# One more seven-product pair in each channel mixer, an accumulating transfer for a second operand sum, and all five engines' orders from one list scheduler

## The chip, the cores and the metric

The kernel runs on one core of a Trainium2 chip. The time is the device time of one execution in microseconds (us); three executions of the kernel before gave 562.88, 563.20 and 563.69 us, so the median is 563.2 us. The engines are named as in the profile: PE (TensorE matmul), PEld (its weight load), DVE (VectorE), ACT (ScalarE), POOL (GpSimd) and SP (SyncE, which here only issues loads).

## The reference

A two-layer decoder trunk on 256 positions of width 1024, in fp32. Layer 0 mixes tokens with a chunked gated MLP, layer 1 with causal attention; in both, four heads attend in parallel to 256 memory tokens. Then each layer has a dense channel mixer:

```python
def swiglu(x, w_in, w_out):
    g, u = jnp.split(x @ w_in, 2, axis=-1)
    return (jax.nn.silu(g) * u) @ w_out

for i in range(DEPTH):                 # 2 layers
    ...                                # mix = gmlp or attention, mem_out = memory attention
    sub = jnp.concatenate([mix, mem_out], axis=-1) @ w_mix_out[i]
    x = layer_norm(ALPHA * x + sub, ln_mix_g[i], ln_mix_b[i])
    x = layer_norm(ALPHA * x + swiglu(x, w_ffn_in[i], w_ffn_out[i]), ln_ffn_g[i], ln_ffn_b[i])
return x
```

The hidden width is 2816, that is 11 chunks of 256 hidden cells; a chunk of `w_in` has 1024 rows and 512 columns (256 for the gate g, 256 for u).

## The kernel before, in words

**Precision.** Every large product is computed from two halves of each operand: ACT writes a rounded `hi` (L248), DVE subtracts it from the source for `lo` (L249), and PE runs three passes, hi·hi, hi·lo and lo·hi, into the same PSUM tile (`PASSES`, L272). So each weight of 128x2048 that comes in by DMA costs two ACT casts and two DVE subtractions of 128x1024, called a split below; the two halves of one weight carry a 0 or a 1 in their name (`spl_s_4_M_0_...` is half 0 or 1 of some product's operand of pair 4; the digit before the last number is the half).

**Channel mixer.** A chunk is computed in one of two ways (`PLANS`, `ffn_steps`). A plain block R multiplies the four row groups of its weight, for both 128-position token tiles: 4x2x3x2 = 48 matmuls of 128x512. A pair S takes two chunks together, cuts positions and rows in two, and computes the 2x2 block product with seven products, M1 to M7, instead of eight: 7x12 = 84 matmuls where two plain blocks take 96. The price is in the operands. Four sums of the token side are made once per layer (`sums`, the tiles `SfM`, `SgM`). On the weight side the host has combined the blocks into four raw tiles per pair, `11`, `12`, `21` and `22`, and four of the seven products need a sum of two of them: M5 = 11+12, M6 adds 22 to that, M7 = 12+22, M4 = 21 + the running sum in 11. The results build up in three PSUM tiles: X takes M1, M6, M7 and M4 one after the other, Y takes M2, Z takes M5 and M3. ACT copies X after M1, Z after M5 and X after M6 to SBUF (`m1`, `m5`, `u2`), DVE adds Y to m1 (L625), Z to u2 (L629) and X to m5 (L632), and after the silu of each half one DVE instruction makes the hidden values (L630, L636). After four transposes per chunk (`transposes`, L658), made during the next block, they are split into `ht` and are the stationary side of the out-product (`chunk_out`, tiles `fof` in layer 0 and `fog` in layer 1).

Before, each layer has three plain blocks and four pairs, and a pair's products run in the order M1, M5, M2, M3, M6, M7, M4. The sums for M5, M6 and M4 are DVE additions of 128x2048 (L199). The sum for M7 is a DMA that POOL issues (L202): it reads `22` from HBM once more and adds it to the `12` in SBUF while writing. All four sums of a layer's token side, and the transposes of the second token tile, stand in the step `x`; in layer 1 the plain blocks 0 and 1 are cut by token tile around it, so that PE has work while the second tile's layer norm runs.

**Order.** Weights come through `Stream`: SP loads raw tiles of 1 MB in the order of use, four rotating buffers and two fixed ones for `11` and `21` (`TAGS`); `make` sums and splits them into ten rotating half tiles (`HALF_BUFS`). PE runs in the order in which the program is written (`manual_schedule`). The other engines are ordered by the framework's scheduler, except for some splits that `stream.behind` holds back.

Of the kernel before, what the change touches and what calls it, by code (L numbers as in the profile page):

```python
# [34 lines left out]
RAW_BUFS = 4  # L35
# [8 lines left out]
PLANS = ((("R", 0), ("R", 1), ("S", 2), ("S", 4), ("S", 6), ("S", 8), ("R", 10)),  # L44
         (("R", 0), ("R", 1), ("R", 2), ("S", 3), ("S", 5), ("S", 7), ("S", 9)))
PRODUCTS = ("M1", "M5", "M2", "M3", "M6", "M7", "M4")

OPERAND = {"M1": ("11", None), "M5": ("11", "12"), "M2": ("21", None), "M3": ("22", None),
           "M6": ("11", "22"), "M7": ("12", "22"), "M4": ("21", "11")}
TAGS = {"11": "gb", "21": "vbig"}  # L50


def ffn_steps(l):

    steps, due, prev = [], [], []
    for kind, c in PLANS[l]:
        new = [("out", p, k, (0, 1)) for p in prev for k in range(2)]
        if kind == "S":


            ins = [("s", c, m) for m in PRODUCTS]
            due += new
            early, due = due[:-3], due[-3:]
            if c == NFF - 2:

                steps += [ins[0], ("tp",), *early, *ins[1:5], due[0], ins[5], ("out", c - 1, 0, (0,)), ("turn", c, 0),
                          ("out", c - 1, 1, (0,)), ins[6]]
                continue
            steps += [ins[0], ("tp",), *early[:1], ins[1], *early[1:], *ins[2:5], due[0], ins[5], due[1], ins[6]]
            due = due[2:]  # L70
        else:
            ins = [("r", c, i, (0, 1)) for i in range(4)]
            if l == 1 and c == 0:

                steps += [*(("r", 0, i, (0,)) for i in range(4)), *(("r", 1, i, (0,)) for i in range(2)), ("x",)]
            elif l == 1 and c == 1:
                steps += [*(("r", 1, i, (0,)) for i in range(2, 4)), *(("r", 0, i, (1,)) for i in range(4)),
                          *(("r", 1, i, (1,)) for i in range(2)), ("tp",), *(("r", 1, i, (1,)) for i in range(2, 4))]
                due += new
            elif c == NFF - 1:  # L80
                steps += [ins[0], ("tp",), *due, *ins[1:], *(("out", NFF - 3, k, (0,)) for k in range(2)), ("tp",)]
            elif c:
                steps += [ins[0], ("tp",), *ins[1:]]
                due += new
            else:
                steps += ins
        prev = [c, c + 1] if kind == "S" else [c]
    return steps


# [971 lines left out]
```

## Time and profile before

The profiled execution has a span of 561.0 us from its first to its last instruction; the three timed executions have a median of 563.2 us. No device time beside the span is given for the profiled execution itself, so the 2.2 us between the two are taken as lying around the span.

| of the span of 561.0 us | busy us | share | instructions |
|---|---|---|---|
| PE | 550.9 | 98% | 3052 |
| PEld | 478.4 | 85% | 3052 |
| DVE | 500.5 | 89% | 667 |
| ACT | 360.1 | 64% | 550 |
| POOL | 22.4 | 4% | 32 |

The granted TensorE clock is 0.998 over the span. Loads that SP issues take 52.8% of the 16 DMA engines' time, the transfers that POOL issues 8.1%. How to read it: PE has work almost without a gap, DVE is full in parts of the span and not in others, so a mean over the span says little of either; each part of the program has to be looked at for itself.

### The profile page before, as it was taken

What the parts mean: (1) busy time and instruction counts of PE and PEld (TensorE: products, weight loads), DVE (VectorE), ACT (ScalarE), POOL (GpSimd) and SP (SyncE); (2) the same over time, 40 slices, a digit from 0 to 9 for tenths busy, and PEclk for the clock granted to TensorE, in tenths of its full rate; (3) what the DMA queues carried; (4) which work ended last, traced back from release to release, by engine and by line L of the source; (5) the groups of instructions that cost most, each with busy time, mean ns of one, the idle gap of its engine ahead of it and who ended that gap; (6) DMA issues with size and microseconds to landing.
All of it is one profiled execution on the core that took longest, in us unless ns stands there. A gap on an engine that the chain in (4) does not pass through costs nothing.

```text
span 561.0 us, 8037 instructions
## 1 busy us (share of the span) xinstructions
PE 550.9 (98%) x3052; PEld 478.4 (85%) x3052; DVE 500.5 (89%) x667; ACT 360.1 (64%) x550; POOL 22.4 (4%) x32
## 2 busy tenths in 40 slices
PE   8999999999999999999999999999999999999994
PEld 8999979888888888888899999788888887888883
DVE  5897999999998999995987879789998997999985
ACT  6766947767655766863466879765676674765910
POOL 2020000000000000000000000000000000000001
PEclk9999999999999999999999999999999999999999
DMA  8997794548756486598477222367258766485602
GB/s 291 399 324 308 250 369 170 208 77 313 210 206 247 112 325 161 192 335 296 140 240 297 75 77 76 142 254 280 85 152 316 197 249 217 133 307 145 225 1 75
DMA packets 21623, 118.88 MB, mean 212 GB/s; under 512 B 2384, under 2 KB 6096, under 8 KB 9168
## 3 DMA queue, kind: packets, MB, share of 16 engines
q1 hardware_dynamic: 20000, 109.45, 52.8%
q0 software_dynamic: 1152, 8.39, 8.1%
q8 instruction: 24, 0.39, 0.3%
q10 hardware_dynamic: 432, 0.52, 0.3%
q14 instruction: 15, 0.12, 0.1%
HBM read 117.31 MB, written 1.05 MB: 211 GB/s over the span
## 4 chain that ended last, share of the span: by engine, by line
PE 85%; DVE 7%; ACT 3%; DMA 2%; issue 2%; SPq 1%; DVEq 0%; ACTq 0%
PE fof L272 11%; PE fog L272 8%; PE Xf L272 8%; PE pg L272 6%; PE pf L272 6%; PE Xg L272 5%; PE opc L272 4%; PE opa L272 4%; PE Zf L272 4%; PE qk L272 4%; PE pu L272 3%; PE bv L272 3%; PE Zg L272 3%; PE pvm L272 3%; PE va L272 2%; PE hkm L272 2%
## 5 line engine op out<-in xcount | busy, mean ns | idle before, releaser
L248 ACT CAST spl_s_M<-raw_s 128x1024 fp32r<-128x1024 f32 x112 | 114.4, 1052 | 56.7 <-DVE raw_s L199 41.9
L249 DVE TENSOR_TENSOR spl_s_M<-raw_s,spl_s_M 128x1024 fp32r<-128x1024 f32 x112 | 132.6, 1217 | 7.7 <-ACT spl_s_M L248 7.5
L272 PE MATMUL fof<-spl_w,htf 128*128 128x512 f32 x264 | 63.8, 392 | 0.0
L272 PE MATMUL fog<-spl_w,htg 128*128 128x512 f32 (+1 forms) x282 | 63.7, 378 | 0.0
L272 PEld LDWEIGHTS fog<-spl_w,htg 128*128 128x128 f32 x282 | 50.2, 188 | 9.4
L272 PEld LDWEIGHTS fof<-spl_w,htf 128*128 128x128 f32 x264 | 49.0, 188 | 10.0
L199 DVE TENSOR_TENSOR raw_s<-raw_s,raw_s 128x2048 f32<-128x2048 f32 x24 | 54.8, 2284 | 0.2
L249 DVE TENSOR_TENSOR spl_w<-raw_w,spl_w 128x1024 fp32r<-128x1024 f32 x44 | 53.0, 1217 | 1.2 <-ACT spl_w L248 1.1
L248 ACT CAST spl_w<-raw_w 128x1024 fp32r<-128x1024 f32 x44 | 45.4, 1050 | 4.7 <-PE fog L272 1.9
L272 PE MATMUL qk<-x2T,spl_qk 128*128 128x256 f32 x288 | 36.3, 283 | 0.0
L272 PEld LDWEIGHTS qk<-x2T,spl_qk 128*128 128x128 f32 x288 | 35.2, 192 | 0.0
L272 PE MATMUL Xf<-spl_s_M,SfM 128*128 128x512 f32 x96 | 23.1, 389 | 0.0
L272 PE MATMUL opc<-spl_o,mix 128*128 128x512 f32 x96 | 23.1, 394 | 0.0
L272 PE MATMUL Zf<-spl_s_M,SfM 128*128 128x512 f32 x96 | 23.1, 389 | 0.0
L272 PE MATMUL Zg<-spl_s_M,SgM 128*128 128x512 f32 x96 | 23.1, 389 | 0.0
L272 PE MATMUL Xg<-spl_s_M,SgM 128*128 128x512 f32 x96 | 23.1, 389 | 0.0
L272 PE MATMUL Xg<-spl_s_M,x3T 128*128 128x512 f32 x96 | 22.7, 391 | 0.2 <-DVE m5g L632 0.2
L272 PE MATMUL Xf<-spl_s_M,x1T 128*128 128x512 f32 x96 | 22.6, 389 | 0.0
L272 PE MATMUL opa<-spl_o,mix 128*128 128x512 f32 x96 | 22.5, 392 | 0.0
L272 PEld LDWEIGHTS Xg<-spl_s_M,x3T 128*128 128x128 f32 x96 | 17.9, 188 | 4.4 <-DVE m5g L632 0.6
L272 PEld LDWEIGHTS Xf<-spl_s_M,SfM 128*128 128x128 f32 x96 | 18.0, 188 | 3.8
L272 PEld LDWEIGHTS Xg<-spl_s_M,SgM 128*128 128x128 f32 x96 | 18.0, 188 | 3.7
(245 smaller groups left out, 1080.2 us busy)
## 6 DMA issues: line engine op xcount, KB each, us to landing
raw_s<-in_w SPq DMA_DIRECT2D x32, 1024.0 KB, 5.1
raw_w<-in_w SPq DMA_DIRECT2D x22, 1024.0 KB, 4.8
raw_o<-in_w SPq DMA_DIRECT2D x8, 1024.0 KB, 6.3
raw_s<-in_w POOLq DMA_DIRECT2D x8, 1024.0 KB, 7.9
raw_r_A<-in_w SPq DMA_DIRECT2D x6, 1024.0 KB, 4.9
raw_r_B<-in_w SPq DMA_DIRECT2D x6, 1024.0 KB, 6.0
raw_qk<-in_w SPq DMA_DIRECT2D x6, 1024.0 KB, 5.5
raw_u<-in_w SPq DMA_DIRECT2D x3, 1024.0 KB, 9.2
```

The costliest lines, as they stand in the source:

```text
L199: self.nc.vector.tensor_add(self.raw[parts[0]], self.raw[parts[0]], self.raw[parts[1]])
L248: nc.scalar.copy(hi, src)
L249: nc.vector.tensor_sub(lo, src, hi.bitcast(F32))
L272: nc.tensor.matmul(o, lhsT, rhs, start=start, stop=stop, skip_group_check=on)
```

## The change

Both layers now have one plain block (chunk 0) and five pairs (1, 3, 5, 7, 9). The order of a pair's products is M1, M5, M2, M6, M3, M7, M4. Of the four weight sums, M5 and M6 stay DVE additions; M7 is still loaded from HBM with an accumulating transfer (now issued when M7's own half is made, not with M5's), and M4 is an accumulating transfer too, from the SBUF tile `11` into the SBUF tile `21`. For the pairs after the first, M1 is copied from X to Y within PSUM and M2 accumulates on top of it, so the silu reads Y and the DVE addition of L625 goes away. A number of copies may run on ACT or on DVE (`nc.copy`, `nc.scale`). The two fixed raw buffers join the rotating ones (six in all), and other tiles that stood in them (x0raw, gv, vn, vt, the layer norm's rows) take such a slot too. Layer 0 now ends as layer 1 did before: on a pair whose second half is turned in the tail (`turn_tile`).

The order of all five engines is now manual. The program is recorded as a list (`Plan.add`); PE keeps the order in which the program is written, `deadlines` works back from it to a latest start for each other instruction, `simulate` lays the instructions out five times with five sets of limits and a table of assumed costs, and the layout in which PE loses least is emitted.

```diff
-RAW_BUFS = 4
+RAW_BUFS = 6
 HALF_BUFS = 10
...
-PLANS = ((("R", 0), ("R", 1), ("S", 2), ("S", 4), ("S", 6), ("S", 8), ("R", 10)),
-         (("R", 0), ("R", 1), ("R", 2), ("S", 3), ("S", 5), ("S", 7), ("S", 9)))
-PRODUCTS = ("M1", "M5", "M2", "M3", "M6", "M7", "M4")
+PLANS = ((("R", 0), ("S", 1), ("S", 3), ("S", 5), ("S", 7), ("S", 9)),) * 2
+PRODUCTS = ("M1", "M5", "M2", "M6", "M3", "M7", "M4")
...
+LOADED = ("M7",)
+MOVED = ("M4",)
...
+        if l == 1 and c == 1:
+
+            first, second = ([("r", 0, i, (tt,)) for i in range(4)] for tt in range(2))
+            steps += [ins["M1"], first[0], ins["M2"], first[1], ("x",), *first[2:], *second, ins["M5"], ("tp",), ins["M6"],
+                      ins["M3"], ins["M7"], due[0], ins["M4"]]
+            due = due[1:]
+        elif c == NFF - 2:
+
+            steps += [ins["M1"], ("tp",), *early, ins["M5"], ins["M2"], ins["M6"], ins["M3"], due[0], ins["M7"],
+                      ("out", c - 1, 0, (0,)), ("turn", c, 0), ("out", c - 1, 1, (0,)), ins["M4"]]
         else:
...
+            n = 2 if early else 1
+            steps += [ins["M1"], ("tp",), *early[:1], ins["M5"], *early[1:], ins["M2"], ins["M6"], ins["M3"], *due[:n - 1],
+                      ins["M7"], due[n - 1], ins["M4"]]
+            due = due[n:]
...
     def make(self):
...
-        if len(parts) == 2 and key[-1] == 0:
+        if key[1] in MOVED and key[-1] == 0:
+            self.nc.gpsimd.dma_start(self.raw[parts[0]], self.raw[parts[1]], accum_op=ALU.add)
+        elif len(parts) == 2 and key[-1] == 0:
             self.nc.vector.tensor_add(self.raw[parts[0]], self.raw[parts[0]], self.raw[parts[1]])
-            if key[1] == "M5":
-                a, b = (f"{key[0]}_{q}" for q in OPERAND["M7"])
-                self.nc.gpsimd.dma_start(self.raw[a], self.unit_ap(b), accum_op=ALU.add)
+        if key[1] in LOADED and key[-1] == 0:
+            a, b = (f"{key[0]}_{q}" for q in OPERAND[key[1]])
+            self.nc.gpsimd.dma_start(self.raw[a], self.unit_ap(b), accum_op=ALU.add)
...
-        tc.manual_schedule(engines={ET.PE}),
+        tc.manual_schedule(engines={ET.PE, ET.DVE, ET.Activation, ET.Pool, ET.SP}),
...
                 if m == "M1":
-                    self.m1 = kept("m1", self.X)
+                    if self.Y.whole:
+                        nc.copy(self.Y, self.X)
+                    else:
+                        self.m1 = kept("m1", self.X)
...
-                    nc.vector.tensor_add(self.m1, self.m1, self.Y)
-                    nc.scalar.activation(self.m1, self.m1, AF.Silu)
+                    if self.Y.whole:
+                        self.m1 = work_tile(f"m1{self.nm}{c}")
+                        nc.scalar.activation(self.m1, self.Y, AF.Silu)
...
                 elif m == "M6":
-                    u2 = kept("u2", self.X)
-                    nc.vector.tensor_add(u2, u2, self.Z)
-                    nc.vector.scalar_tensor_tensor(self.m1, self.m1, -1.0, u2, ALU.mult, ALU.mult)
+                    self.u2 = kept("u2", self.X)
+                elif m == "M3":
+                    nc.vector.tensor_add(self.u2, self.u2, self.Z)
+                    nc.vector.scalar_tensor_tensor(self.m1, self.m1, -1.0, self.u2, ALU.mult, ALU.mult)
...
-            if i == 2:
-                gb = load_gb(1, "mix")
...
+        gb = [load_row(tile_of("act", [P, D], F32, "klm", "g1mix"), 1, "mix_g")]
...
+        gb.append(load_row(tile_of("act", [P, D], F32, "klq", "b1mix"), 1, "mix_b"))
...
+    def either(self, a, b):
+
+        op = self.add(*a)
+        op.other = Op(op.n, *b)
+
+    def copy(self, out, src):
+        self.either(("scalar", "copy", (out, src), {}), ("vector", "tensor_copy", (out, src), {}))
...
+    def deadlines(self):
+        t = 4300
+        for op in self.ops:
+            if op.engine == "tensor":
+                op.late = t
+                t += op.hold
...
+        for op in reversed(self.ops):
+            late = [o.late - self.delay(op, o) for o in op.after if o.late is not None]
+            late += [follow[b].late - self.delay(op, follow[b]) for b in op.roots if b in follow]
+            if op.late is not None:
+                late.append(op.late)
+            op.late = min(late) if late else t
...
+        for trial in self.TRIALS:
...
+            out, lost = self.simulate(*trial)
+            self.trials.append(lost)
+            if best is None or lost < best[0]:
+                best = lost, [(op, op.opens, op.call, op.start, op.end, [b.slot for b in op.opens]) for op in out]
...
+                t0 = min(t for t, _ in c)
+                first = [x for x in c if x[0] <= t0 + 1]
+                t, op = min(first, key=lambda x: (x[1].late, x[1].n))
```

Three places show how the instructions move. The first is POOL over layer 0's channel mixer. Before it issues one transfer per pair, all of them from `in_w` in HBM:

```order
L362 TENSOR_TENSOR rsa_1047<-rsa_1047,mhalf 128x1
L202 DMA raw_s_2_12_1294<-in_w 128x2048
L202 DMA raw_s_4_12_1591<-in_w 128x2048
L202 DMA raw_s_6_12_1826<-in_w 128x2048
L202 DMA raw_s_8_12_2061<-in_w 128x2048
```

Now it issues two per pair, one from `in_w` and one from the SBUF tile `raw_s_..._11`:

```order
L520 TENSOR_TENSOR rsa_1108<-rsa_1108,mhalf 128x1
L520 DMA raw_s_1_12_923<-in_w 128x2048
L520 DMA raw_s_1_21_1006<-raw_s_1_11_870 128x2048
L520 DMA raw_s_3_12_1394<-in_w 128x2048
L520 DMA raw_s_3_21_1432<-raw_s_3_11_1171 128x2048
L520 DMA raw_s_5_12_1644<-in_w 128x2048
L520 DMA raw_s_5_21_1668<-raw_s_5_11_1636 128x2048
```

The second place is DVE towards the end of a pair of layer 0, with the sum for M4 before (pair 4; `raw_s_4_21` is the target, `htf` the split of transposed hidden values, `spl_w` the splits of out-weights):

```order
L249 TENSOR_TENSOR spl_s_4_M_0_1777<-raw_s_4_12_1591,spl_s_4_M_0_1777 128x1024
L249 TENSOR_TENSOR spl_s_4_M_1_1786<-raw_s_4_12_1591,spl_s_4_M_1_1786 128x1024
L249 TENSOR_TENSOR spl_w_3_0_1796<-raw_w_3_1650,spl_w_3_0_1796 128x1024
L199 TENSOR_TENSOR raw_s_4_21_1595<-raw_s_4_21_1595,raw_s_4_11_1589 128x2048
L625 TENSOR_TENSOR m1f_1631<-m1f_1631,Yf_1611 128x512
L249 TENSOR_TENSOR spl_s_4_M_0_1812<-raw_s_4_21_1595,spl_s_4_M_0_1812 128x1024
```

Now, in pair 5, from the split of M2's operand (the last reader of the old `21`) to the first split of the sum that the transfer leaves in the same tile:

```order
L520 TENSOR_TENSOR raw_s_5_11_1636<-raw_s_5_11_1636,raw_s_5_22_1696 128x2048
L520 TENSOR_TENSOR spl_s_5_M_0_1726<-raw_s_5_21_1668,spl_s_5_M_0_1726 128x1024
L520 TENSOR_TENSOR spl_s_5_M_1_1757<-raw_s_5_21_1668,spl_s_5_M_1_1757 128x1024
L520 TENSOR_TENSOR spl_s_5_M_0_1812<-raw_s_5_11_1636,spl_s_5_M_0_1812 128x1024
L520 TENSOR_TENSOR spl_s_5_M_1_1819<-raw_s_5_11_1636,spl_s_5_M_1_1819 128x1024
L520 TENSOR_TENSOR spl_s_5_M_0_1765<-raw_s_5_22_1696,spl_s_5_M_0_1765 128x1024
L520 TENSOR_TENSOR spl_s_5_M_1_1772<-raw_s_5_22_1696,spl_s_5_M_1_1772 128x1024
L520 TENSOR_TENSOR spl_w_3_1_1804<-raw_w_3_1664,spl_w_3_1_1804 128x1024
L520 TENSOR_TENSOR spl_s_5_M_0_1826<-raw_s_5_12_1644,spl_s_5_M_0_1826 128x1024
L520 TENSOR_TENSOR spl_s_5_M_1_1839<-raw_s_5_12_1644,spl_s_5_M_1_1839 128x1024
L520 TENSOR_TENSOR spl_w_4_0_1848<-raw_w_4_1746,spl_w_4_0_1848 128x1024
L520 TENSOR_TENSOR htf_1794<-tpf_1779,htf_1794 128x512
```

The row that follows the last one is `spl_s_5_M_0_1894<-raw_s_5_21_1668`, the split that needs the landed sum. The addition of 128x2048 has gone from between; nine other instructions lie between the second row of `21` and that split.

The third place is PE at the start of layer 1's channel mixer, from the first matmul that needs only the first token tile (`ptc` are the transposes of the second tile, `pg` the plain blocks). Before:

```order
L272 MATMUL pg_3780<-spl_r_0_A_3777,x3T 128x512 x6
L272 MATMUL pg_3780<-spl_r_0_A_3787,x3T 128x512 x6
L272 MATMUL pg_3780<-spl_r_0_B_3798,x3T 128x512 x6
L272 MATMUL pg_3780<-spl_r_0_B_3807,x3T 128x512 x6
L272 MATMUL pg_3826<-spl_r_1_A_3823,x3T 128x512 x6
L272 MATMUL pg_3826<-spl_r_1_A_3833,x3T 128x512 x6
L374 MATMUL ptc_3844<-ident,xres 128x128 x4
L374 MATMUL ptc_3853<-ident,xres 128x128 x4
L272 MATMUL pg_3826<-spl_r_1_B_3882,x3T 128x512 x6
L272 MATMUL pg_3826<-spl_r_1_B_3891,x3T 128x512 x6
```

Now M1 and M2 of pair 1 stand among the pieces of the plain block, and behind the plain block's second tile comes M5 (`Zg`), the first product that needs the token sums `SgM`:

```order
L520 MATMUL Xg_3810<-spl_s_1_M_0_3538,x3T 128x512 x6
L520 MATMUL Xg_3810<-spl_s_1_M_1_3574,x3T 128x512 x6
L520 MATMUL pg_3835<-spl_r_0_A_3703,x3T 128x512 x6
L520 MATMUL Yg_3846<-spl_s_1_M_0_3712,x3T 128x512 x6
L520 MATMUL Yg_3846<-spl_s_1_M_1_3738,x3T 128x512 x6
L520 MATMUL pg_3835<-spl_r_0_A_3753,x3T 128x512 x6
L520 MATMUL ptc_3877<-ident,xres 128x128 x4
L520 MATMUL ptc_3882<-ident,xres 128x128 x4
L520 MATMUL pg_3835<-spl_r_0_B_3763,x3T 128x512 x6
L520 MATMUL pg_3835<-spl_r_0_B_3774,x3T 128x512 x6
L520 MATMUL pg_3908<-spl_r_0_A_3703,x3T 128x512 x6
L520 MATMUL pg_3908<-spl_r_0_A_3753,x3T 128x512 x6
```

Two pieces of `r_0_B` follow, and then `Zg_3955<-spl_s_1_M_0_3805,SgM_3918`. Before, the pieces of two plain blocks for both token tiles and then a whole third plain block stood ahead of the first product on `SgM`; now it is one plain block with M1 and M2.

More of the change, by code (lines that the diff above doesn't have):

```diff
@@ L56, in ffn_steps @@
     for kind, c in PLANS[l]:
[L57 to L70, printed above, removed]
-        else:
[L72 to L86, printed above, removed]
@@ new lines, with __init__ @@
+class Buffer(View):
+    def __init__(self, pool, space, tag, bufs, shape, dtype, name):
+        n = 1
+        for s in shape[1:]:
+            n *= s
+        ap = space[:P * n].rearrange("(p n) -> p n", p=P)
+        if len(shape) > 2:
+            names = "abcd"[:len(shape) - 1]
+            ap = ap.rearrange(f"p ({' '.join(names)}) -> p {' '.join(names)}", **dict(zip(names, shape[1:])))
+        super().__init__(None, ap)
+        self.pool, self.tag, self.bufs, self.dims, self.dtype, self.name = pool, tag, bufs, list(shape), dtype, name
+        self.psum, self.whole = pool == "ps", False
+        self.tile, self.log, self.slot, self.left, self.last = None, [], None, 0, 0.0
@@ new lines, with __init__, calls, cost @@
+class Op:
+    def __init__(self, n, engine, name, args, kw):
+        self.n, self.engine, self.name, self.args, self.kw = n, engine, name, args, kw
+        out = kw["out"] if "out" in kw else args[0]
+        views = [v for v in [*args, *kw.values()] if isinstance(v, View)]
+        self.writes = [v for v in (out, kw.get("accum_out")) if isinstance(v, View)]
+        self.reads = [v for v in views if not any(v is w for w in self.writes)]
+        self.before, self.after, self.opens = {}, [], []
+        self.late, self.other = None, None
+        self.cost()
+    def calls(self):
+        return {o.engine: o for o in (self, self.other) if o}
+    def cost(self):
+        w = max([v.width() for v in self.writes + self.reads] or [1])
+        e, n = self.engine, self.name
+        if n == "dma_start":
+            v = (self.writes or self.reads)[0]
+            self.bytes = 4 * v.ap.ap[0][1] * v.width()
+            self.hold, self.lat = (900 if e == "gpsimd" else 400), 0
+        elif e == "tensor":
+            w = self.args[2].width() if n == "matmul" else P
+            f32 = n == "matmul" and self.args[2].root.dtype == F32
+            self.hold = max(104, (w + 32) / 2.4) if not f32 else 0.85 * w
+            self.lat = 200 + 0.37 * w if not f32 else self.hold + 270
+        elif e == "vector":
+            slow = n in ("tensor_scalar_mul", "tensor_scalar_add") or n == "tensor_copy"
+            self.lat = 225 + 0.48 * w if n == "tensor_scalar_mul" and w > 8 else 150 + 1.042 * w
+            self.hold = self.lat - 82
+        elif e == "scalar":
+            self.lat = 190 + 0.842 * w + (200 if "accum_out" in self.kw else 0)
+            self.hold = self.lat - 100
+        else:
+            self.lat = self.hold = 700 + 2.5 * w if w < 8 else 250 + 2.0 * w
@@ L293, in build @@
             pattern=[[0, 2], [-1, P]], channel_multiplier=1)
-        klm, klq = (const.tile([P, 2, 2, T], F32R, name=n) for n in ("klm", "klq"))
+        klm, klq = (tile_of("act", [P, 2, 2, T], F32R, n, n) for n in ("klm", "klq"))
         for kl in (klm, klq):
@@ L493, in mem_q @@
         def mem_q(name, xs):
-            qa = [actp.tile([P, 2, T], F32R, tag=f"qm{c}", name=f"q{name}{c}") for c in range(2)]
+            qa = [tile_of("act", [P, 2, T], F32R, f"qm{c}", f"q{name}{c}") for c in range(2)]
             t = proj_t(name, xs)
```

443 lines of the change are left out of this document (363 added, 80 removed).

## The prediction

> **What bounds the kernel now.** I read the page's busy line first, then what PE waited for, then the chain of waits for the spacing of PE's work, then the windows for DVE.
>
> ```profile
> span 561.0 us, 8037 instructions
> PE 550.9 (98%) x3052; PEld 478.4 (85%) x3052; DVE 500.5 (89%) x667; ACT 360.1 (64%) x550; POOL 22.4 (4%) x32
> ```
>
> ```profile
> PE warmup L284 <- DVE mhalf L281: 1.1, 1, 1.1
> PE va L272 <- ACT spl_v L248: 0.6, 1, 0.6
> PE s L272 <- DVE klq L480: 0.6, 2, 0.4
> PE Xg L272 <- DVE m5g L632: 0.2, 1, 0.2
> ```
>
> The list of PE's waits has four entries, 2.5 us in all, and the first two belong to the start. PE is the bound: 0.8 us in the middle (0.6 + 0.2) is all that a better order could win back there. What remains is the amount of PE work, and whether the others keep up with less of it. Two stretches of the chain give the price of PE work:
>
> ```profile
> 132.21 2.72 PE Yf L272 x12
> ...
> 153.97 0.87 PE tpf L658 x8
> ...
> 184.79 0.87 PE tpf L658 x8
> ```
>
> Twelve matmuls of 128x512 take 2.72 us, 0.2267 us each. From one pair's transposes to the next pair's are 30.82 us: 7 products and 4 pieces of out-product, 11 x 2.72 + 0.87 = 30.8. So a pair runs on PE with no gap. Beside it stands DVE:
>
> ```profile
> core 0: us, PE busy (x) PEld busy (x) DVE busy (x) ACT busy (x) POOL busy (x), PEclk, DMA share, GB/s
> 140.00:160.00 20.00, 20.00 (x94) 16.67 (x93) 20.00 (x20) 12.75 (x17) 0.87 (x1) 1.00 0.60 164
> 440.00:460.00 20.00, 20.00 (x93) 16.61 (x93) 20.00 (x19) 13.00 (x16) 0.00 (x0) 1.00 0.68 217
> ```
>
> ```profile
> L249 DVE TENSOR_TENSOR spl_s_M<-raw_s,spl_s_M 128x1024 fp32r<-128x1024 f32 x112 | 132.6, 1217 | 7.7 <-ACT spl_s_M L248 7.5
> L199 DVE TENSOR_TENSOR raw_s<-raw_s,raw_s 128x2048 f32<-128x2048 f32 x24 | 54.8, 2284 | 0.2
> L249 DVE TENSOR_TENSOR spl_w<-raw_w,spl_w 128x1024 fp32r<-128x1024 f32 x44 | 53.0, 1217 | 1.2 <-ACT spl_w L248 1.1
> L632 DVE TENSOR_TENSOR m5f<-m5f,Xf 128x512 f32<-128x512 f32 x4 | 2.7, 680 | 0.0
> ```
>
> In the pairs DVE is full as well. Per instruction (busy over count, since neighbours overlap a little) a split is 132.6/112 = 1.184 us, an out-weight split 53.0/44 = 1.205, a weight sum 54.8/24 = 2.28, a 512-wide step 2.7/4 = 0.675. A pair needs 14 splits, 4 out-weight splits, 3 sums and 7 steps: 16.6 + 4.8 + 6.8 + 4.7 = 33.0 us, against PE's 30.8. DVE falls behind by some 2 us per pair and lives on the lead won in the plain blocks (48 matmuls, 10.9 us of PE, for only 4 splits, 4.7 us).
>
> **The change part by part.**
>
> *PE.* A layer goes from 3 x 48 + 4 x 84 to 48 + 5 x 84 matmuls of 128x512: 480 to 468. Over two layers that is 24 fewer, 24 x 0.2267 = **5.44 us less**. Out-products and transposes keep their number.
>
> The Trainium skill ("Perfetto Trace Analysis", Identifying the Most-Contended Engine) says that matmul busy time judges TensorE badly and weight-load busy time should be used. The row for that is
>
> ```profile
> L272 PEld LDWEIGHTS fof<-spl_w,htf 128*128 128x128 f32 x264 | 49.0, 188 | 10.0
> ```
>
> and by it 24 matmuls would be worth 24 x 0.188 = 4.5 us; the starts in the chain above are 0.2267 apart with no gap, so the trace goes with 5.44.
>
> *Waits in the middle.* The 0.6 us on klq and the 0.2 on m5g came from DVE's order. The new order has every latest start in view; I take back all of it, **-0.8** (bounds 0 and -0.8).
>
> *DVE inside a pair.* One sum fewer (M4, -2.28), the addition of Y gone (-0.675), and a copy here and there that was ACT's (about half a step per pair): 21.4 + 2 x 2.28 + 6.5 x 0.675 = 30.4 us, against 30.8. So five pairs in a row, with no plain block between to recover, should hold with 0.4 us to spare each, where the old load would have lost 5 x 2.2 = 11 us of lead. This is the step on which the gain stands. Price 0. Bounds: 0, and 2.7 (the new order has 15 copies on DVE where there were 6; five of the nine are counted here, the other four at 0.675 could fall where DVE has no lead). ACT is 64% busy, and its 14 added casts hide in its idle third:
>
> ```profile
> L248 ACT CAST spl_s_M<-raw_s 128x1024 fp32r<-128x1024 f32 x112 | 114.4, 1052 | 56.7 <-DVE raw_s L199 41.9
> ```
>
> Without that cover each would cost 1.05 us.
>
> *The transfers of the sums.* Per pair POOL now issues two, and they have these rows:
>
> ```profile
> raw_s<-in_w POOLq DMA_DIRECT2D x8, 1024.0 KB, 7.9
> ...
> q1 hardware_dynamic: 20000, 109.45, 52.8%
> q0 software_dynamic: 1152, 8.39, 8.1%
> ```
>
> ```profile
> 146.19 0.87 POOL L202 DMA_DIRECT2D raw_s<-in_w  x1 [30.53 <-DVE raw_s L199]
> ```
>
> ```profile
> DMA to landing us min/median/max: 7.8/7.9/9.0
> ```
>
> M7's sum has some 15 DVE instructions between its release and its first split, about 17 us against 0.9 + 7.9: safe. For M4 the transfer may start when M2's split has read the old `21`, and must have landed for the split nine DVE instructions later (the second place of the order): 8 splits and one `htf`, 8 x 1.184 + 0.675 = 10.1 us, against 0.9 of issue and 7.9 of landing. The margin is **1.3 us**. An accumulating transfer out of SBUF is not in this trace; the nearest row is the one from HBM, 7.8 to 9.0. I take 7.9, so price 0. The DMA engines have room: a load of 1 MiB costs 2.84 us of them (52.8% of 561.0 over 109.45 MB), an accumulating one 5.68 (8.1% over 8.39 MB), so a pair used 6 x 2.84 + 5.68 = 22.7 of its 30.8 us and will use 28.4, 92%. That leaves room, but a load that meets both will land later than now. Bounds: 0, and 2.0 us per pair (rival C).
>
> *Start of layer 1's channel mixer.* One plain block instead of three has to cover the second tile's layer norm and the token sums.
>
> ```profile
> 374.37 0.87 PE ptc L374 x8
> 377.98 8.17 PE pg L272 x36
> 386.15 0.87 PE ptc L374 x8
> ```
>
> ```profile
> L366 DVE SCALAR_TENSOR_TENSOR xres<-xres,rsc,gb1mix 128x512 f32<-128x512 f32 x4 | 2.8, 745 | 0.0
> L353 DVE BATCH_NORM_STATS2 stc<-xres 128x6 f32<-128x512 f32 x4 | 2.6, 679 | 0.0
> L596 DVE TENSOR_TENSOR hg<-hg,pg 128x256 f32<-128x256 f32 x6 | 2.5, 414 | 0.2
> ```
>
> Count from the first matmul on the first tile alone (377.98 now). A piece of six is 8.17/6 = 1.36. M1, piece, M2, piece, transposes, two pieces, four pieces of the second tile: 2.72 + 1.36 + 2.72 + 1.36 + 0.87 + 2.72 + 5.44 = 17.2. Then M5, four transposes, M6, M3 and M7's first half: M7's second half is due at 27.15. By then DVE has to do the layer norm (five of 0.70, two of 0.65, small ones: 5.0), 10 splits (11.8), a weight sum (2.3), 12 steps (8.1) and two `hg` (0.8): 28.0. Short by about **1.0**, and I take that. Bounds: 0 (if copies go to ACT), and 3.0 (four more 0.675 steps of the sums on DVE's path). Layer 0's start has no such squeeze: its whole first block is plain and the same work stands behind both tiles; 0.
>
> *Hand-offs.* At a pair's end the silu of X, the product with m5 and the transposes must fit behind the next M1, 2.72 us; one of them already shows a wait.
>
> ```profile
> 473.33 0.61 DVE m5g L632
> 473.98 5.74 PE Xg L272 x24
> ```
>
> There are ten of them now and eight before. New is the copy of X into Y, which must be there before M2 writes on it: M5 and an out-product piece lie between, at least 2.72 us, for one step of about 0.7, on ACT or DVE. If that cover is gone, PE waits the step itself. I take **0.5** for all hand-offs; bounds 0 and 5.6 (a 0.7 step late in each of the eight pairs with such a copy).
>
> *Ends and start.* Layer 0 now ends in a turned half, as layer 1 does, where PE runs through without a wait:
>
> ```profile
> 536.41 2.74 PE Xg L272 x12
> 539.15 2.72 PE fog L272 x12
> 542.31 11.18 PE fog L272 x66
> ```
>
> Between the last two rows lie 0.44 us, four transposes at 0.11. Price 0; if the second half's split came late there, one step of 0.675 is the bound. The tail behind it is unchanged in its steps. At the start SP's loads stand in another order (v1's first piece ahead of v0's last half): 0, bounds 0.6 either way, the size of PE's wait for spl_v above. The rows for layer 1's first norm are loaded later, into space of klm and klq:
>
> ```profile
> gb1mix<-in_ln_mix_b SPq DMA_DIRECT2D x1, 512.0 KB, 4.9
> ```
>
> A landing of 4.9 us is covered by the six out-product pieces ahead of the close, over 8 us; 0.
>
> *Sum on the span:* 561.0 - 5.44 - 0.8 + 1.0 + 0.5 = 556.3, that is 4.7 less. The median of the runs is 2.2 above the span, so 563.2 - 4.7 = **558.5 us**.
>
> **The rivals.**
>
> *A, the forecast:* PE stays the bound, DVE just holds. Own range 556.5 (no loss at all: 563.2 - 6.2 = 557.0, and the 0.6 of the start) to 560.5 (the bounds of start and hand-offs half used).
>
> *B, the gain is half eaten by order.* DVE is strict in its order and 99% full (30.4 of 30.8) for five pairs; a late cast or landing now has no plain block behind it to make up for. For it: DVE's rows are 7.5 us idle behind ACT's casts in `spl_s_M` alone, 7.5/112 = 0.07 us each, 0.9 us per pair if they lay inside the pairs, which is more than the spare 0.4: 10 x 0.5 = 5 us less what the lead of ten half tiles buffers. Against: those waits fell mostly where DVE was ahead. Half of it, 2.5 us, gives 561.0.
>
> *C, slower: M4's transfer lands late.* Place: the pairs. DVE stops at the split of `21`, and everything behind it (the next pair's splits, then PE) moves. The point from which it decides: the 10.1 us less 0.9 of issue allow a landing of 9.2; DVE's spare of 0.4 makes it 9.6; and ten half tiles, worth 1.36 us of PE each, hold some 10 us of lead at the start of a layer's pairs, 2 us for each of the five, so 11.6. For it: two loads ahead of it in the DMA engines would make 7.9 + 2 x 2.84 = 13.6, and loads do spread:
>
> ```profile
> DMA to landing us min/median/max: 4.7/5.9/9.0
> ```
>
> Then a pair loses 13.6 - 11.6 = 2.0; in four of the ten pairs 8.0: 561.0 + 8.0 - 5.4 - 0.8 + 1.0 = 563.8 on the span, **566**. Against: the eight POOL transfers land within 7.8 to 9.0, with the DMA engines 0.60 to 0.68 busy in the windows above.
>
> The Trainium skill ("SBUF — State Buffer", two separate sides) warns of a trap in which a DVE instruction holds the port that GpSimd needs to write descriptors, so that transfers issued by POOL wait. The issues here took 0.87 us in a stretch where DVE was 20.00 of 20.00 busy, so the trace does not bear it out for these DVE instructions; what would be added is at most one DVE instruction, 1.2 to 2.3 us, per issue.
>
> *D, no change:* the new order keeps DVE too far ahead or behind at the layers' starts (3.0) and the hand-offs lose 2.5: 557.0 + 5.5 = 562.5.
>
> **How the numbers follow.** A 0.62, B 0.18, C 0.13, D 0.07. The time is A's, 558.5. The range leaves A's lower edge in and goes up through B and D to the lower part of C: 556.0 to 565.0; beyond it lies most of C. The measurement can tell 0.2%, 1.1 us, from no change, so faster is below 562.1: A and nearly all of B and a little of D, 0.78. The same is D's middle and B's end, 0.08; slower, above 564.3, is C and D's upper end, 0.14.
>
> **What would show it.** 24 fewer PE matmuls and a PE busy time near 545.5; no entry above 0.5 us in PE's waits except the start's, one at `Zg` or `Xg` of layer 1's first pair of about 1 us. DVE near 20 of 20 in every window of the pairs, and at most small waits of DVE on a transfer. Landing of POOL's transfers at 8 to 9 us. Wrong is the forecast if PE waits in the later pairs of a layer for splits (B), if ACT or DVE wait for `raw_s` DMAs and landings reach 11 us (C), or if the PE spacing in the pairs is no longer 2.72 per product.

## The result, and the profile after

The changed kernel takes 570.3 us, the kernel before 563.45 us beside it: ratio 1.0141, 95% interval 1.0111 to 1.0171. It is slower by 6.9 us where 4.7 us less was forecast; the median lies above the stated range (556.0 to 565.0). The profiled execution has a span of 568.1 us, 7.1 more than before.

The page of the changed kernel, as of before: the span and the busy time of each engine.

```profile
span 568.1 us, 8070 instructions
PE 550.0 (97%) x3028; PEld 475.2 (84%) x3028; DVE 506.1 (89%) x674; ACT 370.8 (65%) x563; POOL 32.7 (6%) x44
```

PE has the 24 matmuls less (3052 to 3028), but its busy time fell by 0.9 us, not by 5.4. So PE now waits, and some of its matmuls run slower. The list of PE's waits (what PE waited for: us in total, times, longest) says where:

```profile
PE tpg L520 <- DVE m5g L520: 2.9, 3, 2.0
PE tpf L520 <- DVE m5f L520: 1.5, 1, 1.5
PE qk L520 <- DVE mix L520: 1.2, 1, 1.2
PE tpf L520 <- DVE hf L520: 1.2, 1, 1.2
PE Xf L520 <- DVE m5f L520: 1.2, 1, 1.2
PE warmup L674 <- DVE mhalf L671: 1.1, 1, 1.1
PE Zg L520 <- DVE htg L520: 0.6, 1, 0.6
PE tpg L520 <- DVE m1g L520: 0.6, 1, 0.6
```

Before, the list had four entries and 2.5 us; now it has ten and 11.0 us. Seven of the eight shown are new, and six of them are hand-offs of the channel mixer: the transposes `tpf` and `tpg` wait for the hidden values m1, m5 and hf, the next products for what is made of them.

The first matmul of each stage in the two traces shows in which stage the 12.5 us went (7.1 more, where 5.4 less of work is done). The channel mixers have 2.72 us less work each.

| stage | before, us | after, us | lost against its work |
|---|---|---|---|
| up to layer 0's channel mixer | 101.07 | 101.70 | 0.6 |
| layer 0's channel mixer | 174.78 | 177.14 | 5.1 |
| layer 1's attention | 101.97 | 102.41 | 0.4 |
| layer 1's channel mixer, to the end of PE's last matmul | 175.66 | 179.80 | 6.9 |
| the tail behind PE | 7.49 | 7.01 | -0.5 |

What is late for the hidden values is seen in the chain of waits of the changed kernel, here through a pair of layer 1 (start, us, what):

```profile
459.80 2.28 DVE spl_s_M L520 x2
...
462.71 7.74 DMA raw_s<-raw_s
...
471.28 10.39 DMA raw_s<-in_w
...
484.62 1.05 ACT spl_s_M L520
485.67 0.49 ACT sgg L520
...
486.19 0.70 DVE m5g L520
486.89 0.05 issue
486.93 0.98 PE tpg L520 x7
```

Read it from above: DVE splits M2's operand; that releases M4's transfer (7.74 us); its landing frees a raw slot, for which SP has a load waiting; that load lands 10.39 us after its issue; its casts stand on ACT ahead of the silu `sgg`; the product m5 comes after that, and PE's transposes wait. One turn of this loop, from the silu at 452.36 to the one at 485.67, is 33.3 us; PE's work in that turn (seven products, four pieces of out-product and the transposes) is 30.8.

The loads are issued in bursts behind M4's transfer, and they land later. The page's DMA issues before had 5.1 us for `raw_s` and 4.8 for `raw_w`; now:

```profile
raw_s<-in_w SPq DMA_DIRECT2D x40, 1024.0 KB, 7.6
raw_w<-in_w SPq DMA_DIRECT2D x22, 1024.0 KB, 8.6
raw_s<-in_w POOLq DMA_DIRECT2D x10, 1024.0 KB, 9.0
raw_s<-raw_s POOLq DMA_DIRECT2D x10, 1024.0 KB, 7.7
```

ACT's waits for the loads of a pair before were 5.0 us in all, 1.6 the longest (and 0.9 for those of the out-weights, `raw_w`):

```profile
ACT spl_s_M L248 <- DMA raw_s<-in_w: 5.0, 5, 1.6
```

In the changed kernel they are:

```profile
ACT spl_s_M L520 <- DMA raw_s<-in_w: 25.1, 15, 3.9
ACT spl_w L520 <- DMA raw_w<-in_w: 16.0, 6, 4.3
...
ACT spl_s_M L520 <- DMA raw_s<-raw_s: 8.5, 6, 2.4
```

ACT's row of instructions shows what that does to the silu (start, us, then what it waited for in brackets):

```profile
479.29 1.05 ACT L520 CAST spl_w<-raw_w 128x1024 fp32r<-128x1024 f32 x1 [4.07 <-DMA raw_w<-in_w]
481.77 3.90 ACT L520 CAST spl_s_M<-raw_s 128x1024 fp32r<-128x1024 f32 x4 [1.42 <-DMA raw_s<-in_w]
485.57 0.58 ACT L520 ACTIVATE sgg<-Xg 128x512 f32<-128x512 f32 x1
```

ACT idles 4.07 and 1.42 us for loads and then has four casts to do. PE reaches the transposes at 486.0, one product (2.72 us) after M4's last matmul; the silu of M4's result starts only at 485.57.

### The profile page after: what moved, and what is told of

The parts are those of the page before. It is cut to its first block, busy times and chain, and to the rows that moved or that the text cites. A ratio compares the mean times of both kernels' runs of the same rounds, so it can differ in the third digit from the quotient of the medians.

```text
span 568.1 us, 8070 instructions
## 1 busy us (share of the span) xinstructions
PE 550.0 (97%) x3028; PEld 475.2 (84%) x3028; DVE 506.1 (89%) x674; ACT 370.8 (65%) x563; POOL 32.7 (6%) x44
## 3 DMA queue, kind: packets, MB, share of 16 engines
HBM read 119.41 MB, written 1.05 MB: 212 GB/s over the span
## 5 line engine op out<-in xcount | busy, mean ns | idle before, releaser
L520 ACT CAST spl_s_M<-raw_s 128x1024 fp32r<-128x1024 f32 x140 | 139.8, 1050 | 53.4 <-DMA raw_s<-in_w 25.1
L520 DVE TENSOR_TENSOR spl_s_M<-raw_s,spl_s_M 128x1024 fp32r<-128x1024 f32 x140 | 164.4, 1219 | 7.2 <-ACT spl_s_M L520 7.0
L520 DVE TENSOR_TENSOR raw_s<-raw_s,raw_s 128x2048 f32<-128x2048 f32 x20 | 45.7, 2284 | 0.0
L520 PE MATMUL Xf<-spl_s_M,x1T 128*128 128x512 f32 x120 | 28.4, 391 | 1.3 <-DVE m5f L520 1.2
L520 PE MATMUL Zg<-spl_s_M,SgM 128*128 128x512 f32 x120 | 29.0, 390 | 0.6 <-DVE htg L520 0.6
L520 PE MATMUL Zf<-spl_s_M,SfM 128*128 128x512 f32 x120 | 29.0, 390 | 0.0
L520 PE MATMUL Xg<-spl_s_M,SgM 128*128 128x512 f32 x120 | 29.0, 390 | 0.0
L520 PE MATMUL Xf<-spl_s_M,SfM 128*128 128x512 f32 x120 | 28.8, 389 | 0.0
L520 PEld LDWEIGHTS Xf<-spl_s_M,x1T 128*128 128x128 f32 x120 | 22.4, 188 | 6.7 <-ACT spl_s_M L520 1.6
L520 PEld LDWEIGHTS Zg<-spl_s_M,SgM 128*128 128x128 f32 x120 | 22.5, 188 | 5.7 <-DVE htg L520 1.1
## 6 DMA issues: line engine op xcount, KB each, us to landing
raw_u<-in_w SPq DMA_DIRECT2D x3, 1024.0 KB, 10.1
```

The source lines that it names most:

```text
L520: getattr(getattr(self.nc, c.engine), c.name)(*map(real, c.args), **{k: real(v) for k, v in c.kw.items()})
```

## The experiments

The letters in the expectations stand for theories, not for the prediction's rivals: L, the loads are slowed by the bytes of the second transfer; M, M4's own landing is late (rival C); D, DVE is too full; O and R, the order that was fixed in advance, and that it was made with transfer times too short; G, a loop through the raw slots; S, the scheduler by itself.

**One transfer shortened, the order of every engine kept.** In `emit`, for M4 (and in the second run for M7):

```diff
+            args = [real(x) for x in c.args]
+            if "accum_op" in c.kw and isinstance(c.args[1], View):
+                args = [x[:, :64] for x in args]
```

> The changed kernel with the order of every engine kept word for word, but the transfer that makes M4's sum moves 64 of its 2048 columns (so M4's products are computed from an incomplete sum). Theory L (the second accumulating transfer fills the DMA engines, the loads of SP land in up to 10.8 us in place of 5, and the casts that wait for them stand in ACT's fixed order ahead of the silu, so the hidden values come late for PE's transposes): the engines are as free as before, loads land in 5 to 6 us, the waits at tpf and tpg go, 561 to 563 us. Theory M (rival C as predicted: M4's own landing is what comes late): also 561 to 563, since nothing of size lands. Theory D (DVE is too full or badly ordered, no transfer matters): 569 to 571.

> The changed kernel with the same order on every engine, M4's transfer whole, but the one that makes M7's sum moves 64 of 2048 columns (M7's products are computed from an incomplete sum). It frees as much of the DMA engines as the run with the short M4 transfer, but leaves M4's landing as it is. Theory L: 561 to 564 us, nearly as much is won back. Theory M: 569 to 571, M4 lands as late as it did. Theory D: 569 to 571.

Measured: 564.57 us without M4's bytes (ratio to before 1.0031, 1.0019 to 1.0043), 570.12 us without M7's (1.0129, 1.0104 to 1.0154). The same bytes leave the DMA engines in both, and only M4's pay: 5.7 us. So theory L, that the bytes as such slow the loads, falls; what counts in this order is the time from M4's release to its landing, with what the landing sets free. M7's transfers land after up to 11.9 us in the changed kernel, and that costs nothing measurable. D falls as the only cause too.

**M4's sum back on DVE**, `MOVED = ()`.

> The changed kernel with M4's sum back on DVE as an addition of 128x2048, planned anew: one accumulating transfer per pair as before, but DVE gets 2.28 us more per pair, 32.7 against PE's 30.8. Theory L: loads land in 5 to 6 us again, and five pairs lose 1.9 us each less the lead of about 8 us per layer: 560 to 566 us. Theory M: the same. Theory D: DVE is already too full, so slower than the changed kernel, 573 to 580.

Measured: 574.41 us (1.0205, 1.019 to 1.0221), the value that theory D named. DVE's busy time rises from 506.1 to 525.0 us, and that costs more than the transfer does: in an order made with the same assumed costs, five pairs in a row need the 2.28 us taken off DVE.

**One assumed cost.** The order is made from a table in which a transfer of b bytes occupies the DMA engines for b/437 ns, 2.40 us for 1 MiB, and a POOL transfer 2.1 times that. In the trace, five loads issued behind M4's transfer landed over 13.7 us, 2.74 each.

```diff
-                size = op.bytes * (2.1 if e == "gpsimd" else 1) / 437
+                size = op.bytes * (2.1 if e == "gpsimd" else 1) / 380
```

> The changed kernel with one number of the planner's assumed costs set to what the trace shows: a transfer's time in the DMA engines from bytes/437 to bytes/380 ns (2.76 us for a load of 1 MiB where five loads in a row landed 2.74 us apart). Only the order on DVE and ACT changes. Theory L: casts of late loads are put behind the silu where that costs nothing, a third to two thirds of the waits at the transposes go: 564 to 568 us. Theories M and D: 569 to 571, no change.

Measured: 563.95 us (1.0011, 0.9997 to 1.0025). Nothing but the order on DVE and ACT (with one copy that changes from DVE to ACT, and one load's place) differs, the same transfers run and land nearly as late (`raw_s` 7.3 and `raw_w` 8.4 us by the median), and 6.4 us are back. ACT waits for the loads of the pairs about as long as before: 14.5 and 25.6 us for `raw_s` and `raw_w`, against 25.1 and 16.0. So these 6.4 us are not the price of late landings as such, nor of ACT's idle time; they are the price of an order made for earlier landings.

**The silu moved by hand.** In the changed kernel's order, each silu goes ahead of the casts that stand directly before it.

```diff
+        todo = self.order()
+        for s in [op for op in todo if op.engine == "scalar" and op.name == "activation" and op.args[2] == AF.Silu]:
...
+                todo.remove(o)
+                todo.insert(todo.index(s) + 1, o)
```

> The changed kernel with PE's, DVE's, POOL's and SP's orders kept word for word; on ACT each silu is moved ahead of up to four weight casts that stood directly before it and on which nothing in between depends (23 places, mostly one cast). No transfer changes. Theory O (ACT's fixed order: casts that wait for late loads or stand in a run hold up the silu): the silu comes about 1.05 us earlier at each of the five worst places, 3 to 5 us are won: 565 to 567. Theory M (M4's own landing comes late and moves all behind it, whatever ACT's order): 569 to 571.

Measured: 575.36 us (1.0228, 1.0199 to 1.0257), 5 us slower where 3 to 5 faster was expected. ACT now stands at the silu until PE has X (16.7 us for `sgg`, 3.9 in the changed kernel), and the casts behind it come late:

```profile
ACT sgg L532 <- PE Xg L532: 16.7, 3, 7.6
...
ACT m1f L532 <- PE Yf L532: 11.8, 4, 4.2
...
ACT m1f L532 <- DVE m1f L532: 7.4, 1, 7.4
```

So "casts ahead of the silu" is not the fault in itself. An engine that runs in a fixed order loses in both directions; the right place of the silu depends on when the loads land.

**Three plain blocks and four pairs under the new scheduler**, with M4's sum on DVE and by transfer: `PLANS` and `ffn_steps` of before.

> The new scheduler with the plan of before: three plain blocks and four pairs per layer (in the old sequence of blocks, the ends of layer 0 as before), M4's sum on DVE; M7 loaded and M1 copied in PSUM as in the changed kernel. So the scheduler without the fifth pair and without the second transfer. If the fifth pair and the transfer are what costs (theories M and O): 563 to 565, the plain blocks give the slack back. If the scheduler's order by itself costs (theory S): 567 to 571.

> As the run with three plain blocks and M4 on DVE, but M4's sum by the accumulating transfer: the second transfer without the fifth pair. Theory M: the late landing costs in each of eight pairs, 565 to 569, slower than with M4 on DVE. Theory O: the plain blocks and the DVE time freed (2.28 us per pair) give slack, the same as with M4 on DVE or up to 2 us less, 562 to 565.

Measured: 566.17 us (1.0054, 1.0039 to 1.0069) and 565.91 us (1.0048, 1.0033 to 1.0063). First, the new scheduler (with what came with it: M1's copy in PSUM, M6 ahead of M3, six shared slots) costs 3.1 us, more than theories M and O said and less than S. PE's waits of the run with M4 on DVE:

```profile
PE va L529 <- ACT spl_v L529: 1.5, 1, 1.5
PE qk L529 <- DVE mix L529: 1.2, 1, 1.2
PE warmup L683 <- DVE mhalf L680: 1.1, 1, 1.1
PE tpg L529 <- DVE hg L529: 0.7, 1, 0.7
PE tpf L529 <- DVE hf L529: 0.6, 1, 0.6
```

None is a wait for a pair's own products: they are the start, the attention and the hidden values of a plain block. Second, with three plain blocks the transfer costs nothing: 565.91 lies in theory M's range, but M had it slower than with M4 on DVE, and it is not. From there the fifth pair costs 8.2 us with M4 on DVE (574.41) and 4.4 with the transfer (570.3), where the work falls by 5.4.

**The second transfer alone, in the kernel before with its old scheduler.**

```diff
+            if key[1] == "M4":
+                self.nc.gpsimd.dma_start(self.raw[parts[0]], self.raw[parts[1]], accum_op=ALU.add)
+            else:
+                self.nc.vector.tensor_add(self.raw[parts[0]], self.raw[parts[0]], self.raw[parts[1]])
```

> The kernel before, its plan and its scheduler, with one edit: M4's sum by POOL's accumulating transfer from 11 onto 21 in place of DVE's addition of 128x2048. If the transfer itself harms (theory M): 566 to 571, eight pairs wait for its landing. If only the five pairs and the order made for them harm (theories O, R): PE was the bound, DVE only gets 2.28 us per pair free: 562 to 564.

Measured: 590.82 us (1.05, 1.0484 to 1.0516), 28 us slower, 3.5 per pair, far beyond every theory. PE's and ACT's waits in it:

```profile
PE Xf L275 <- ACT u2f L620: 9.3, 4, 3.9
PE Xg L275 <- ACT u2g L620: 5.1, 2, 3.4
...
ACT spl_s_M L251 <- DVE raw_s L202: 30.5, 11, 4.6
ACT spl_s_M L251 <- DMA raw_s<-raw_s: 17.1, 5, 6.2
```

ACT's wait for the sums on DVE is not new (41.9 us in the kernel before). New are its wait for the landing and PE's for `u2`, the copy of X that M7 needs. In two of layer 0's pairs the cast that waits for the landing stands ahead of this copy on ACT: it waits 6.18 us until 211.17 and 4.99 until 247.93, the copies start at 213.59 and 250.77, and PE waits 1.52 and 3.85 for them. The same transfer is free in the run with three plain blocks under the new scheduler (565.91 beside 566.17). It lands after 11.3 us by the median here and 7.1 there, so what it meets on the DMA engines differs too. How the 28 us split between the later landing and the place of the cast was not separated.

**The raw slots.** M4's block `21` added from HBM onto the sum in `11`, which frees the slot of `21` early; and seven raw slots for six, with nine half tiles for ten.

```diff
-           "M6": ("11", "22"), "M7": ("12", "22"), "M4": ("21", "11")}
-LOADED = ("M7",)
-MOVED = ("M4",)
+           "M6": ("11", "22"), "M7": ("12", "22"), "M4": ("11", "21")}
+LOADED = ("M7", "M4")
+MOVED = ()
```

> The changed kernel with M4's sum taken the other way round: POOL adds the block 21 from HBM onto the running sum in the SBUF tile 11 (as it does for M7), in place of adding 11 onto 21 within SBUF. As many transfers of the same size; planned anew with unchanged costs. The slot of 21 is free after M2's split, some 10 us before the transfer lands. Theory G (a loop through the raw slots sets a pair's period: M4's transfer holds the slots of 11 and 21, the next loads are issued only when it lands, land up to 10.4 us later, then casts, silu, product, splits, the next M4 transfer; 33.3 us from one silu to the next, 452.36 to 485.67, against 31.7 of PE's work with an out-product more): one load in five goes out early, 564 to 567. Theory R (only that the order was made for landings 2 us too early, whatever holds the slots): 569 to 571.

> The changed kernel with seven raw slots in place of six and nine half tiles in place of ten (both do not fit); planned anew with unchanged costs. Theory G: the loads of the next pair no longer wait for M4's landing, 564 to 567, unless the lost half tile (1.36 us of lead) takes it back, up to 570. Theory R: no gain, 570 to 573.

Measured: 577.93 us (1.0275, 1.0256 to 1.0294) and 566.05 us (1.0053, 1.0033 to 1.0074). The seventh slot wins back 4.3 us, as theory G said, in an order made with the old assumed cost; the order on DVE and ACT is another one too, so the slot alone is not shown to do it. The transfer from HBM loses 7.6, outside what either theory named: it may start only after M6's splits, two later than M2's, and from HBM a median of 9.0 us passes to the landing in place of 7.7. ACT's casts wait 33.5 us for POOL's transfers (13.4 in the changed kernel). The splits that need these casts hold up DVE's addition of X to m5 (at 446 to 450 us, for one), and PE then waits at the start of M4, which writes on X:

```profile
PE Xg L520 <- DVE m5g L520: 4.4, 5, 1.7
PE Xf L520 <- DVE m5f L520: 4.3, 3, 2.1
```

That is once more the time from M4's release to its landing, and it speaks against theory G in the form in which the slot of `21` matters. (The 31.7 us in the expectation are not borne out: the turn from 452.36 to 485.67 holds 30.8 us of PE's work.)

**M2 early.** Assumed cost /380, and the products in the order M1, M2, M5, M6, M3, M7, M4, with an out-product between M1 and the transposes.

```diff
-            steps += [ins["M1"], ("tp",), *early[:1], ins["M5"], *early[1:], ins["M2"], ins["M6"], ins["M3"], *due[:n - 1],
+            steps += [ins["M1"], *early[:1], *(ins[m] for m in ("M2", "M5")[:not early]), ("tp",), *(ins[m] for m in ("M2", "M5")[not early:]),
+                      *early[1:], ins["M6"], ins["M3"], *due[:n - 1],
```

> The changed kernel with the planner's transfer rate as measured (bytes/380, as in the run with that change alone, 563.95 us) and another order of a pair on PE: M1, one old out-product, the transposes, M2, M5, M6, M3, M7, M4 (before: M1, the transposes, one out-product, M5, M2, M6, M3, M7, M4); in layer 0's first pair the transposes come after M2 and M5. The hand-off from silu to transposes then has 5.4 us of PE work as cover in place of 2.7, and M4's transfer may start earlier, since M2's operand is split earlier. If the hand-off's cover is what is short (theory O): the remaining gaps at tpf, tpg and Xf (4 to 5 us in the run with the rate alone) go, 558 to 560. If not: 563 to 565.

Measured: 562.99 us (0.9998, 0.9985 to 1.0011). The entries at `tpf` and `tpg` are gone from PE's waits, but only 1.0 us of the 4 to 5 came back, which is within the spread of the runs (561.6 to 564.3 here, 562.1 to 566.0 with the cost alone). With the transfer from HBM, with the other order in layer 1's second pair too, and with a seventh slot:

> The run with the measured transfer rate and M2 early (562.99 us), with M4's sum made onto 11 from HBM as well. Theory G: another 1 to 2 us, 560.5 to 562. Theory R: as without, 562.5 to 563.5.

> The run with M2 early and M4's sum from HBM, and in layer 1's second pair the transposes ahead of the first out-product (M1, M2, transposes, out-product, M5), since the run with M2 early had its longest wait in a pair there (PE 1.0 us for an out-weight split, at 425). 0.5 to 1 us less than without, 560 to 561.5; no change if DVE is what is late there and the wait only goes to the next instruction.

> The run with the measured rate and M2 early (562.99 us) with seven raw slots and nine half tiles. Theory G (the slots still bind): 560 to 562. If the order was all: no gain, 563 to 566 because a half tile of lead is lost.

Measured: 575.48 us (1.0235, 1.0214 to 1.0256), 575.43 us (1.0223, 1.0204 to 1.0243) and 564.66 us (1.003, 1.0019 to 1.004). The transfer from HBM harms here as well. The seventh slot, worth 4.3 us in the bad order, now costs 1.7: in this order a slot more wins nothing. The 1.7 may be the lost half tile (1.36 us of lead); no run has the one without the other.

**How much slack.** The assumed cost at /345 (3.04 us for 1 MiB) and /300 (3.50 us), with M2 early; /345 without; and /345 with M2 early and the other order in layer 1's second pair.

> The run with the measured rate and M2 early, with the assumed transfer time longer than measured (bytes/345 in place of /380: 3.04 us for 1 MiB). If the order is still made for landings that come too late now and then (the spread of its ten runs was 561.6 to 564.3): 560.5 to 562 and a narrower spread. If landings are right now: 562.5 to 564.

> M2 early and bytes/300 (3.50 us for 1 MiB, a quarter longer than measured). If more slack helps still: 560 to 561.2. If the order now puts casts so late that DVE waits for them: 562 to 566.

> The changed kernel with one number changed: assumed transfer time bytes/345 in place of bytes/437. With bytes/380 it took 563.95 us; with M2 early besides, /380 gave 562.99 and /345 gave 561.43. If the slack in the order is what pays: 561.5 to 563, most of the way without M2 early. If M2 early is needed for it: 563.5 to 565.

> M2 early and bytes/345 (561.43 us), and in layer 1's second pair M1, M2, transposes, out-product, M5. If the 1.0 us that PE waits there for an out-weight split can be covered: 560.3 to 561. If DVE is behind there as a whole, the wait moves on to the next product: 561.2 to 562.

Measured, in this order: 561.43 us (0.9972, 0.9961 to 0.9983), 573.72 us (1.0196, 1.0182 to 1.021), 562.01 us (0.9973, 0.9962 to 0.9984) and 561.22 us (0.9966, 0.9953 to 0.9978). The changed kernel with nothing but /345 is 8.3 us faster than the changed kernel, and faster than the kernel before. ACT's row at the place shown above, in that run:

```profile
474.34 1.05 ACT L520 CAST spl_w<-raw_w 128x1024 fp32r<-128x1024 f32 x1 [4.12 <-DMA raw_w<-in_w]
477.30 0.60 ACT L520 ACTIVATE sgg<-Xg 128x512 f32<-128x512 f32 x1 [1.91 <-PE Xg L520]
477.79 1.99 ACT L520 CAST spl_s_M<-raw_s 128x1024 fp32r<-128x1024 f32 x2
```

ACT still waits 4.12 us for the same kind of load, but the silu comes straight behind it and starts the moment X is there. PE's waits in that run:

```profile
PE qk L520 <- DVE mix L520: 1.2, 1, 1.2
PE tpf L520 <- DVE hf L520: 1.2, 1, 1.2
...
PE tpg L520 <- DVE m1g L520: 0.6, 1, 0.6
...
PE tpg L520 <- DVE m5g L520: 0.3, 1, 0.3
```

The waits for m5 are down from 5.6 us to 0.3. In five of the ten pairs (140.6 to 233.1 and 449.0 to 510.6 us) PE is busy for 154.1 of 154.1 us and DVE for 146.9. At /300 the time is far beyond both expectations. The order puts casts so late that the other side fails, and 5.0 us of the loss stand in two entries of PE's waits:

```profile
PE Xg L521 <- DVE spl_s_M L521: 2.7, 4, 0.8
PE Xf L521 <- DVE spl_s_M L521: 2.3, 3, 0.8
```

The other order in the second pair takes its 1.0 us wait for `spl_w` away, and 0.7 comes back as a wait for the copy into Y: 561.22 beside 561.43, within the spread.

## Why the prediction was wrong, point by point

**PE's work** was right: 24 matmuls fewer, and 2.72 us for twelve where PE does not wait.

**The waits in the middle, "I take back all of it, -0.8"** failed, and in sign. It assumed that an order with every latest start in view is at least as good as the old one. With what came with it the new scheduler costs 3.1 us (566.17 beside 563.09), in hand-offs that I never priced because the edits did not touch them: 1.2 us at `qk` for `mix`, 0.6 and 0.7 at a plain block's hidden values, some at the start.

**DVE inside a pair** was right: with the assumed cost at /345 five pairs run through with 29.4 us of DVE's work on the mean in 30.8, against the 30.4 counted, and with the old 32.7 (M4 on DVE) the changed kernel is 4.1 us slower still. But that ACT's "idle third" covers its casts was read from a mean over the span, and it does not hold at the pair's end.

**M4's transfer, "price 0", is the first step that failed in the sum.** The landing was sized well (7.7 us, against 7.9 taken), but the margin of 1.3 us was counted on DVE alone. The split of `21` begins with a cast on ACT of 1.05 us, which must come first; so 10.1 - 1.05 - 8.8 leaves 0.25. ACT waited for this landing in six of ten pairs, 8.5 us. And the slots that the transfer holds were not in the sum at all: the next loads are issued at its landing, all together, and land up to 11.0 us later.

**Hand-offs, "0.5 in all", is the second, and the larger.** The waits of PE for m5, m1, hf and `ht` are 8.0 us in the list above, and in the profiled execution a slowed clock (below) adds 1.7 on PE. The clock alone does not make the time: executions with a mean granted clock of 0.996 and 0.997 took 569.79 and 570.75 us, the profiled one with 0.992 took 569.85, and the fourth with 0.990 took 574.02. The bound of 5.6 that I kept was nearer the truth than the value, by luck: it was worked out for the copy of X into Y, for which PE never waits. I priced the hand-off by its own steps (a silu, a product) and not by what stands ahead of them on ACT: casts that wait for a load. Three runs show the cause from both sides. With the order kept and M4's bytes taken away, 5.7 us come back (564.57); with the transfers kept and the order made with another assumed transfer time, 6.4 (2.76 us for 1 MiB, 563.95) and 8.3 (3.04 us, 562.01) of the 12.5. So the cause is an order fixed in advance with 2.40 us per load where a burst takes 2.74, 1.7 us late by its fifth load. Each assumed cost gives one order, so a part of 6.4 or 8.3 may be the chance of that order. The last 4.8 us to the full 557.2 (563.45 less 5.44 and 0.8) are partly the scheduler's 3.1: but for 0.9 us at the end of layer 1's first pair, PE's waits at /345 lie outside the pairs. How the rest splits stays open.

**Layer 1's start, +1.0**, came out near in size, but not in its place: no product of the first pair waits for a split. DVE's lateness shows behind it, 0.6 at `tpg` for m1, 0.3 for m5 and 0.6 at `Zg` for `htg`, all at the hand-off.

**The rivals.** C named the place (M4's transfer) and the side, and with 566 it came nearest, at less than half the loss; its mechanism was wrong: the landing was not stretched to 13.6 us by loads ahead of it (M4's ten transfers took 7.0 to 8.0), the loads behind it were. B had the mechanism, an order without slack in which a late cast has no plain block behind it, but at 2.5 us. Both are parts of the loop shown above, and I gave it 0.31 in two halves. The trap that the Trainium skill ("SBUF — State Buffer", two separate sides) describes played no part: POOL's twenty issues took 0.85 to 0.90 us, the first 1.03, and seventeen of them stood beside a DVE that was busy throughout.

## What to carry to other kernels

Where every engine's order is fixed in advance, a wait is paid by whatever stands behind it, so price a hand-off by the instructions ahead of it on each of its engines (the cast as well as the subtraction, the load as well as the cast), and follow a new transfer on to the slots it holds and the loads that these release. The assumed costs of a list scheduler are part of the kernel: set transfer times from landings measured in the bursts they will come in, try values on both sides (2.40 us gave 570, 2.76 gave 564, 3.04 gave 562, 3.50 with M2 early gave 574), and judge the plan, the transfer and the scheduler in separate runs, since the transfer cost nothing in one order and 28 us in another.

## What the runs showed of the hardware that I had not expected

PE's clock fell after a short wait. In the changed kernel PE waited 2.0 us for m5g from 451.6 on, and then ran at about half speed: the granted clock was 0.5 for 3.4 us from 453.7 on (a table by windows of the changed kernel; the column after the five engines' busy times is the granted clock):

```profile
core 0: us, PE busy (x) PEld busy (x) DVE busy (x) ACT busy (x) POOL busy (x), PEclk, DMA share, GB/s
448.00:453.00 5.00, 3.64 (x17) 2.73 (x15) 2.33 (x4) 3.57 (x5) 0.85 (x1) 1.00 1.02 301
453.00:457.00 4.00, 3.37 (x12) 2.98 (x13) 4.00 (x5) 4.00 (x6) 0.00 (x0) 0.59 1.03 258
457.00:462.00 5.00, 5.00 (x24) 4.14 (x23) 5.00 (x5) 4.54 (x6) 0.00 (x0) 0.99 0.35 138
```

The seven transposes and five matmuls behind the wait came at twice their spacing or near it, 1.7 us more than the wait itself. The wait of 1.5 us at 170.3 left the clock at 1.00. The Trainium skill ("TensorE: Matmul & The Clock Gate", What's actually happening) puts the fall at an idle window of about 3.4 us; here a pause of 2.0 us was followed by it. The length of the pause alone does not decide: in other runs 2.4 us (the transfer from HBM with M2 early, at 482.2), 2.5 (the silu moved, at 489.6) and 3.4 (the second transfer in the kernel before, at 520.8) left the clock at 1.

An accumulating transfer from SBUF to SBUF landed in 7.7 us by the median, sooner than the one from HBM (9.0) in the same kernel. That is no rule: with the second transfer in the kernel before it was 11.3 against 8.3. Five loads issued behind such a transfer landed up to 10.8 us after their issue, where the quickest load of the same size in this kernel took 4.7.
